# Block sums in the delta rule, scalings on one engine, and splits handed out as steps, in a hybrid decoder layer

## The chip, the core and the metric
The kernel runs on one core of one Trainium2 chip. The metric is device time in microseconds (us), the median of three runs: 1703.05 us before the change (1699.76 to 1704.30). Five engines work side by side, each through its own queue of instructions in order: TensorE (PE, with its weight loads shown apart as PEld), VectorE (DVE), ScalarE (ACT), GpSimd (POOL) and SyncE (SP), which here only issues DMA transfers.

## The reference
One layer on x (1024 tokens by 1024 channels, float32):

```python
proj = x @ w_in                                # q k v z beta a | NSA q, k/v, gates | merge gates
o_a  = gated_deltanet(...)                     # 4 heads, delta rule in chunks, state S 128x128
o_b  = native_sparse_attention(...)            # 8 heads of 64, 2 kv heads: compressed, selected, window
mixed = sigmoid(gate_a) * (o_a @ w_branch_gdn) + sigmoid(gate_b) * (o_b @ w_branch_nsa)
h    = layer_norm(alpha * x + mixed @ w_out)
u    = causal_dwconv(h @ w_up)                 # 2 x 2816 channels, 3 taps
f    = (silu(u_g) * u_v) @ w_down              # w_down: 2816 x 1024
out  = layer_norm(alpha * h + f)
```

The selected branch takes 16 blocks of 64 keys, and there are 16, so it is plain causal attention. Each of its softmaxes, and each of the window's, ends with P = exp(s - max) times a number per row, the gate divided by the row's sum.

## The kernel before
The stages follow one another in the trace: a first projection (0 to 60 us), the delta rule (60 to 593), attention (593 to 864), the branch products, merge and output projection (864 to 1104), the feed-forward part (1104 to 1655) and the last norm. Products take a float32 operand as two parts, high and low, one from a copy on ACT (`wh`, `oAh`, ...) and the other from a subtraction (`wl`, `oAl`, ...).

**Delta rule.** Eight iterations n = 0 to 7, each half a head (head n // 2, four chunks of 128 tokens). `pre` (L543) prepares a half: it forms `Am`, writes it to DRAM (`aimg`, L588), reads its diagonal blocks back as `AB` (L590), inverts them in small DVE instructions (L596 to L612, `pr`, `XB`), writes that to DRAM (`zimg`, L613) and reads it back as `Z` (L615), whose transpose `X` (L617) goes into the products `sm<-Z,Am` that follow. `scan` (L678) carries the state `S` from chunk to chunk (L703). Between these steps PE's order is filled with projections (`fills`, L759 to L772): `plan` names for each n its generators (`z_gen`, `act_gen`, `mix_gen`), each of which loads a weight block of 512 KB (L189), splits it on ACT and POOL (L183, L184), and gives 48 matmuls. `mix_gen` writes its result as `sig` to DRAM (L537).

**Attention.** Sixteen units (t, g), a tile of 128 queries by a kv head. For a unit `score_steps` (L945) makes scores and their exponentials `P` for branch b = 0 (selected) and 1 (window): DVE takes the row maxima (L979), ACT the exponentials with their sums (L981), and `fin` makes `rr` = gate / sum on DVE (`norm`, L942 and L943) and calls `scale` (L928) four times, once a head. `scale` goes round the letters of `SCALE = "GGGGGA"` (L926): G is a multiplication on POOL (L934), A one on ACT (L932). `cmp_scores` does the same for the compressed branch, `Pc`, always with POOL (L1010). `pv_steps` (L1013) turns P with PE (L1045), copies it out of PSUM as high part on ACT (L1052) and low part on DVE (L1053), and multiplies by `vS`; its end takes a buffer `tmp`, from ACT (L1029), and adds on DVE into `oB` (L1030). `weave` mixes the score steps of one unit with the product steps of the one before.

**Down sums.** The feed-forward part reads sums of blocks of w_down. `down_sums` (L1075) makes them and puts them into DRAM (`wsum`): a call finishes the block that the last call began (three POOL subtractions, L1079 and L1081, and two stores of 256 KB, L1083) and begins the next (two loads of 256 KB, L1090). There are 22 blocks; the attention loop calls it 25 times, once or twice a unit. Its buffers, `tmp`, the weight blocks and the mask tile `am` are all tiles "w" of the pool `stream`, a ring of three; `am` holds one of the three for all of attention.

**Splits of oA.** `gA` holds the result of the gated delta rule. `split_high` (L1106) copies it in eight pieces, four on ACT and four on DVE, and `split_low` (L1116) subtracts in eight pieces on POOL, before the branch products. Both are called in the attention loop, in the units (0, 0) and (0, 1), the loop's last two (`UNITS` has t = 0 at its end).

**What sets the order.** Only PE's instructions run in the order in which the program issues them (`MS`, L26). Those of DVE, ACT, POOL and SP are put in order by a scheduler that plays the program on a timeline of its own when the kernel is built, so the place of a call in the code doesn't by itself say where its instructions come in a queue.

Of the kernel before, what the change touches and what calls it, by code (L numbers as in the profile page):

```python
# [11 lines left out]
F32 = mybir.dt.float32  # L12
F32R = mybir.dt.float32r
# [134 lines left out]
def hybrid_block_kernel(ctx: ExitStack, tc: tile.TileContext, x, w_in, gdn_conv_w, gdn_a_log,  # L148
# [341 lines left out]
    sig = [dram.tile([128, T], F32, name=f"sig{j}") for j in range(16)]  # L490
    gd = tc.tile_pool(name="gdn", bufs=2)
    with gd as gp:
# [247 lines left out]
        with tc.manual_schedule(engines=MS):  # L740
# [186 lines left out]
    SCALE = "GGGGGA"  # L927
# [147 lines left out]
    def down_sums():  # L1075

        if held:
            b, k, cs = held.pop()
            G.tensor_tensor(b[:, 0:2], b[:, 1:4:2], b[:, 0:2], op=OP.subtract)  # L1079
            for o, x, y in ((3, 3, 0), (2, 2, 3)):  # L1080
                G.tensor_tensor(b[:, o], b[:, x], b[:, y], op=OP.subtract)  # L1081
            for r in range(2):
                nc.sync.dma_start(wsum[r][k].rearrange("p (h c) -> p h c", h=2)[:, :, cs], b[:, 2 * r:2 * r + 2, :])  # L1083
        if summed:
            k, c = divmod(summed.pop(0), 2)
            cs = slice(c * 256, c * 256 + 256)
            b = wtile().rearrange("p (b c) -> p b c", b=4)
            for r in range(2):
                src = w_down[(k + KD * r) * 128:(k + KD * r + 1) * 128, :].rearrange("p (h c) -> p h c", h=2)
                nc.sync.dma_start(b[:, 2 * r:2 * r + 2, :], src[:, :, cs])  # L1090
            held.append((b, k, cs))

# [13 lines left out]
    def split_high(src, nm_, pool, engines):  # L1106
        hi = oT[nm_, "hi"] = pool.tile([128, 4, T], F32R, name=f"o{nm_}h", tag="s")
        for hf, hs in enumerate(HS):
            oT[nm_, "h", hf] = hi[:, :, hs]
            for k in range(4):  # L1110
                if engines[k % len(engines)] is V:
                    V.tensor_copy(hi[:, k, hs], src[:, k, hs])
                else:
                    A.activation(hi[:, k, hs], src[:, k, hs], AF.Copy)

    def split_low(src, nm_, pool, engine):  # L1116
        hi = oT[nm_, "hi"]
        lo = pool.tile([128, 4, T], F32R, name=f"o{nm_}l", tag="s")
        for hf, hs in enumerate(HS):
            oT[nm_, "l", hf] = lo[:, :, hs]  # L1120
            for k in range(4):
                engine.tensor_tensor(lo[:, k, hs], src[:, k, hs], hi[:, k, hs].bitcast(F32), op=OP.subtract)
# [18 lines left out]
    with tc.manual_schedule(engines=MS):  # L1141
# [4 lines left out]
        for t, g in UNITS[1:]:  # L1146
            s = stats(t, g)
            down_sums()
            if (t, g) == (0, 0):
                split_high(gA, "A", S6, [A, V])  # L1150
            if (t, g) == (0, 1):
                load_ab(0, wtile)
                split_low(gA, "A", S6, G)
            weave(score_steps(s, 0), pairs[:n0])
            cmp_scores(s)
            if t > 2:
                down_sums()
            weave(score_steps(s, 1), pairs[n0:])
# [69 lines left out]
        split_high(oB, "B", S2b, [A, V])  # L1228
        split_low(oB, "B", S2b, V)
# [694 lines left out]
```

## Time and profile before

| | |
|---|---|
| median of three runs | 1703.05 us |
| profiled execution | 1698.21 us, span 1696.5 us, granted clock 0.992 |
| PE | busy 1660.5 us, 98% of the span |
| DVE, ACT, POOL | busy 1115.9, 734.3, 777.5 us |
| delta rule, 60 to 593 us | PE busy 531.84 of 533.00 |
| attention, 593 to 864 us | PE busy 257.32 of 271.00, DVE 233.94, ACT 210.97, POOL 186.23 |
| feed-forward, 1104 to 1655 us | PE busy 551.00 of 551.00 |

The windows view gives for a stretch each engine's busy time with the number of its instructions, and the clock that TensorE was granted as a share of full speed (PEclk). The timeline gives each instruction's start and length, and in brackets how long its engine stood idle ahead of it and which instruction, by engine, tile and line, ended that. An idle time on an engine that isn't the bottleneck costs nothing.

### The profile page before, as it was taken

The page shows a single profiled execution, that of the slowest core. Times are in us where ns is not written, and L with a number is a line of the kernel's source. Part 1 is how long each engine was busy: PE and PEld are TensorE (multiplying, and loading weights), DVE is VectorE, ACT ScalarE, POOL GpSimd, SP SyncE. Part 2 cuts the span into 40 slices and gives each one's busy share as a digit, 9 for nine tenths or more (in the row PEclk, how much of TensorE's full clock was granted, in tenths as well). Part 3 has the DMA queues.
Part 4 walks back from the last instruction along what each step waited for, and adds up shares of the span by engine and source line. Part 5 has one row for each costly group of instructions (what it writes and reads, how often), then busy time and mean ns, then how long its engine had stood idle before and what let it go on. Part 6 is the DMA issues. An engine that isn't in the chain of part 4 may idle for free.

```text
span 1696.5 us, 23194 instructions
## 1 busy us (share of the span) xinstructions
PE 1660.5 (98%) x8453; PEld 1391.9 (82%) x8453; DVE 1115.9 (66%) x2108; ACT 734.3 (43%) x1268; POOL 777.5 (46%) x630
## 2 busy tenths in 40 slices
PE   9999999999999999999899998999999999999997
PEld 9788888888888887888787887788888888888886
DVE  4555657567523478999853338997777677865657
ACT  3322322333223477888733215544444444444333
POOL 2322222222213647778647326778777777110005
PEclk9999999999999999999999999999999999999999
DMA  5222221212222313333036603334322332697722
GB/s 180 76 64 77 58 75 46 77 52 60 87 73 61 119 37 115 127 123 107 13 106 209 232 25 116 90 105 132 105 93 100 105 107 93 218 331 264 233 91 99
DMA packets 199022, 189.85 MB, mean 112 GB/s; under 512 B 19656, under 2 KB 155005, under 8 KB 198909
## 3 DMA queue, kind: packets, MB, share of 16 engines
q1 hardware_dynamic: 198909, 188.39, 34.3%
q8 instruction: 66, 1.08, 0.3%
q14 instruction: 47, 0.39, 0.1%
HBM read 136.97 MB, written 51.38 MB: 111 GB/s over the span
## 4 chain that ended last, share of the span: by engine, by line
PE 80%; DVE 9%; ACT 3%; issue 3%; POOL 2%; DMA 2%; SPq 0%; ACTq 0%; POOLq 0%; DVEq 0%
PE pq L194 35%; PE big L194 30%; PE sm L194 12%; DVE st L979 2%; PE sm L1045 1%; ACT P L981 1%; DVE wh L1053 1%; DVE wl L1053 1%; DVE st L943 1%; POOL P L934 1%; DMA w<-in_w_out_dram 0%; DVE wb L1516 0%; PE big L260 0%; POOL h L1373 0%; POOL h L1374 0%
## 5 line engine op out<-in xcount | busy, mean ns | idle before, releaser
L184 POOL TENSOR_TENSOR wl<-w,wh 128x1024 fp32r<-128x1024 f32 x48 | 115.9, 2417 | 361.2 <-PE big L194 138.6
L194 PE MATMUL big<-xTh,wh 128*128 128x512 f32 x608 | 244.4, 403 | 1.1 <-DVE sil L524 1.1
L194 PE MATMUL big<-xTl,wh 128*128 128x512 f32 x608 | 243.0, 400 | 0.0
L194 PE MATMUL pq<-wd 128*128 128x512 f32 x924 | 209.6, 389 | 0.0
L194 PEld LDWEIGHTS pq<-wd 128*128 128x128 f32 x924 | 173.4, 188 | 36.0
L194 PE MATMUL pq<-xb,wb 128*128 128x512 f32 x792 | 187.6, 391 | 2.1 <-DVE accs L1527 1.5
L1527 DVE SCALAR_TENSOR_TENSOR accs<-pq,fcw,accs 128x510 f32<-128x510 f32 (+3 forms) x264 | 144.5, 568 | 61.0 <-ACT accs L1615 56.3
L194 PEld LDWEIGHTS pq<-xb,wb 128*128 128x128 f32 x792 | 148.5, 188 | 34.9 <-issue 2.9
L194 PE MATMUL big<-xTh,wl 128*128 128x512 f32 x608 | 164.7, 401 | 0.0
L194 PEld LDWEIGHTS big<-xTh,wh 128*128 128x128 f32 x608 | 114.6, 189 | 21.8 <-ACT sil L521 1.5
L194 PEld LDWEIGHTS big<-xTl,wh 128*128 128x128 f32 x608 | 114.6, 189 | 20.5 <-issue 0.2
L194 PE MATMUL pq<-mTh,wb 128*128 128x512 f32 x528 | 126.3, 395 | 3.5 <-ACT mTh L1315 3.1
L194 PE MATMUL pq<-mTl,wb 128*128 128x512 f32 x528 | 127.4, 391 | 0.0
L194 PEld LDWEIGHTS big<-xTh,wl 128*128 128x128 f32 x608 | 109.9, 188 | 21.0
L934 POOL TENSOR_TENSOR P<-P,st 128x640 f32<-128x640 f32 (+6 forms) x94 | 106.4, 1161 | 42.7 <-DVE st L943 16.5
L194 PEld LDWEIGHTS pq<-mTh,wb 128*128 128x128 f32 x528 | 100.2, 190 | 25.7 <-ACT mTh L1315 3.3
L194 PEld LDWEIGHTS pq<-mTl,wb 128*128 128x128 f32 x528 | 99.1, 188 | 21.2
L1516 POOL TENSOR_TENSOR wb<-w,wb 128x512 fp32r<-128x512 f32 x79 | 103.6, 1317 | 27.5 <-ACT wb L1315 27.5
L183 ACT ACTIVATE wh<-w 128x1024 fp32r<-128x1024 f32 x48 | 50.5, 1058 | 115.7 <-PE big L194 62.6
L194 PE MATMUL big<-kS,qS 128*128 128x320 f32 (+5 forms) x384 | 87.6, 345 | 2.1 <-ACT P L981 1.8
L1315 ACT ACTIVATE wb<-w 128x512 fp32r<-128x512 f32 x85 | 53.3, 629 | 80.3 <-PE pq L194 75.9
L979 DVE TENSOR_REDUCE st<-big 128x1 f32<-128x640 f32 (+7 forms) x88 | 83.4, 947 | 6.4 <-PE big L194 6.1
(409 smaller groups left out, 3483.7 us busy)
## 6 DMA issues: line engine op xcount, KB each, us to landing
w<-in_w_in_dram SPq DMA_DIRECT2D x40, 512.0 KB, 3.8
w<-in_w_up_dram SPq DMA_DIRECT2D x36, 512.0 KB, 3.7
w<-in_w_down_dram SPq DMA_DIRECT2D x53, 256.0 KB, 3.8
wsum<-w SPq DMA_DIRECT2D x44, 256.0 KB, 2.4
sig<-th SPq DMA_DIRECT2D x32, 256.0 KB, 2.2
w<-sig SPq DMA_DIRECT2D x30, 256.0 KB, 3.2
wx<-in_w_up_dram SPq DMA_DIRECT2D x11, 512.0 KB, 3.8
gdrC<-accs SPq DMA_DIRECT2D x11, 512.0 KB, 2.6
```

The costliest lines, as they stand in the source:

```text
L183: A.activation(wh[:, :n], w[:, :n], AF.Copy)
L184: G.tensor_tensor(wl[:, :n], w[:, :n], wh[:, :n].bitcast(F32), op=OP.subtract)
L194: PE.matmul(o, a, b, start=start, stop=stop, skip_group_check=True)
L934: G.tensor_tensor(p, p, r.to_broadcast([128, p.shape[1]]), op=OP.mult)
L943: V.tensor_tensor(s["rr"][:, b], s["rr"][:, b], s["gt"][:, b], op=OP.mult)
L979: V.reduce_max(nm, pv if m > 1 else pv[:, 0], axis=AX.X, negate=True)
L981: A.activation(P[:, r0 + i, :n], pv[:, i], AF.Exp, bias=nm[:, i:i + 1], accum_out=su[:, i:i + 1])
L1045: PE.transpose(tp[:n, r * 128:(r + 1) * 128], P[:, r, c0:c0 + n], ident)
L1053: V.tensor_tensor(pl, tp[:n], ph.bitcast(F32), op=OP.subtract)
L1315: A.activation(o, i, AF.Copy)
L1516: e.tensor_tensor(H.tile[:, 1], src(), H.tile[:, 0].bitcast(F32), op=OP.subtract)
L1527: V.scalar_tensor_tensor(o, i, fcw[:, 2 - s, j:j + 1], o, op0=OP.mult, op1=OP.add)
```

## The change
Three parts. The program calls `down_sums` from the delta rule's fills, for n of 1 and more ahead of each generator (by the plan 4, 3, 4, 3, 3, 3, 3 and 2 calls, 25 in all, of which 23 have work), and no longer in the attention loop. `SCALE` becomes "G", so every scaling is a POOL instruction. And `split_high` and `split_low` return lists of steps, which for oA are strewn among the product steps of the same two units, in place of being called at once.

```diff
                 total = 48 * len(fills)
 
-                def chain(fills=fills):
-                    for f in fills:
+                def chain(fills=fills, n=n):
+                    for i, f in enumerate(fills):
+                        if n:
+                            down_sums()
                         yield from f()
...
-    SCALE = "GGGGGA"
+    SCALE = "G"
...
-    def down_sums():
-
-        if held:
-            b, k, cs = held.pop()
-            G.tensor_tensor(b[:, 0:2], b[:, 1:4:2], b[:, 0:2], op=OP.subtract)
-            for o, x, y in ((3, 3, 0), (2, 2, 3)):
-                G.tensor_tensor(b[:, o], b[:, x], b[:, y], op=OP.subtract)
-            for r in range(2):
-                nc.sync.dma_start(wsum[r][k].rearrange("p (h c) -> p h c", h=2)[:, :, cs], b[:, 2 * r:2 * r + 2, :])
...
     def split_high(src, nm_, pool, engines):
-        hi = oT[nm_, "hi"] = pool.tile([128, 4, T], F32R, name=f"o{nm_}h", tag="s")
-        for hf, hs in enumerate(HS):
...
+        return [functools.partial(f, hf, k) for hf in range(2) for k in range(4)]
...
+    def strewn(steps, more):
+
+        out, n = [], 0
+        for i, f in enumerate(steps):
+            out.append(f)
+            while n < len(more) and n * len(steps) < (i + 1) * len(more):
+                out.append(more[n])
+                n += 1
+        return out + more[n:]
...
             s = stats(t, g)
-            down_sums()
+            pa, pb = pairs[:n0], pairs[n0:]
             if (t, g) == (0, 0):
-                split_high(gA, "A", S6, [A, V])
+                pa = strewn(pa, split_high(gA, "A", S6, [A, V]))
+                lows = split_low(gA, "A", S6, G)
+                pb = strewn(pb, lows[:4])
             if (t, g) == (0, 1):
                 load_ab(0, wtile)
-                split_low(gA, "A", S6, G)
-            weave(score_steps(s, 0), pairs[:n0])
+                pa = strewn(pa, lows[4:])
+            weave(score_steps(s, 0), pa)
             cmp_scores(s)
-            if t > 2:
-                down_sums()
-            weave(score_steps(s, 1), pairs[n0:])
+            weave(score_steps(s, 1), pb)
```

PE's queue is the same, instruction for instruction, in both kernels. On SP, the queue at the delta rule's iteration n = 4, before: `w<-in_w_in_dram` is a weight block of a fill, `aimg` to `Z` are the four transfers of `pre`.

```order
L537 DMA sig_638<-th 128x512 x2
L189 DMA w<-in_w_in_dram 128x8x128
L588 DMA aimg_502<-Am 128x4x128
L590 DMA AB<-aimg_502 32x16x16
L189 DMA w<-in_w_in_dram 128x8x128
L613 DMA zimg_500<-XB 32x16x16
L615 DMA Z<-zimg_500 128x4x128
L537 DMA sig_639<-th 128x512 x2
```

The same stretch of SP's queue after the change, where `w<-in_w_down_dram` are the two loads of a block and `wsum_8` its two stores:

```order
L555 DMA sig_638<-th 128x512 x2
L506 DMA w<-in_w_down_dram 128x2x256 x2
L606 DMA aimg_502<-Am 128x4x128
L499 DMA wsum_8_618<-w 256x1x256
L499 DMA wsum_8_629<-w 256x1x256
L608 DMA AB<-aimg_502 32x16x16
L189 DMA w<-in_w_in_dram 128x8x128
L506 DMA w<-in_w_down_dram 128x2x256 x2
L631 DMA zimg_500<-XB 32x16x16
L633 DMA Z<-zimg_500 128x4x128
L499 DMA wsum_8_618<-w 256x1x256
L499 DMA wsum_8_629<-w 256x1x256
```

Two blocks' loads and stores have come in among the four transfers, one pair of stores between `aimg` and `AB`; such a pair, or one store of it, stands there for n = 1 to 5, and all 22 blocks are through before n = 6.

On ACT in the middle of attention, before (around 805 us), where `P<-P` at L932 is a scaling:

```order
L1052 ACTIVATE wh<-sm 128x512
L981 ACTIVATE P_7595,st<-big,st 128x640
L1052 ACTIVATE wl<-sm 128x512
L981 ACTIVATE P_7595,st<-big,st 128x640
L1052 ACTIVATE wh<-sm 128x512
L932 ACTIVATE P_7595<-P_7595,st 128x640
L1052 ACTIVATE wh<-sm 128x512
L981 ACTIVATE P_7696,st<-big,st 128x1024
```

The same stretch after:

```order
L1072 ACTIVATE wh<-sm 128x512
L1001 ACTIVATE P_7608,st<-big,st 128x640
L1072 ACTIVATE wl<-sm 128x512
L1001 ACTIVATE P_7608,st<-big,st 128x640
L1072 ACTIVATE wh<-sm 128x512 x2
L1001 ACTIVATE P_7701,st<-big,st 128x1024
```

The scaling is gone from between the copies. On POOL at the end of attention, before, where `oAl` are the low parts of oA:

```order
L934 TENSOR_TENSOR P_7852<-P_7852,st 128x640 x4
L934 TENSOR_TENSOR Pw<-Pw,st 128x128 x3
L1122 TENSOR_TENSOR oAl<-gA,oAh 128x512 x8
L1010 TENSOR_TENSOR Pc<-Pc,st 128x256
L934 TENSOR_TENSOR Pw<-Pw,st 128x128 x3
```

After:

```order
L954 TENSOR_TENSOR P_7852<-P_7852,st 128x640 x4
L954 TENSOR_TENSOR Pw<-Pw,st 128x128 x4
L1130 TENSOR_TENSOR oAl<-gA,oAh 128x512 x8
L1030 TENSOR_TENSOR Pc<-Pc,st 128x256
L954 TENSOR_TENSOR Pw<-Pw,st 128x128 x4
```

The eight low parts stand in one piece as before, between the same scalings, which are four and four in place of three and three. On ACT the four `oAh` copies, and on DVE the four casts, stand together at the same place as before too.

## Rows read from the trace of the kernel before

**Rows 1.** Windows: busy PE, PEld, DVE, ACT, POOL; PEclk; DMA share; GB/s

```profile
60.00:593.00 533.00, 531.84 (x2867) 446.73 (x2866) 293.45 (x770) 163.64 (x258) 144.78 (x85) 1.00 0.24 69
593.00:864.00 271.00, 257.32 (x1639) 223.93 (x1638) 233.94 (x414) 210.97 (x475) 186.23 (x194) 0.97 0.26 86
660.00:670.00 10.00, 7.83 (x32) 6.52 (x31) 5.74 (x11) 5.21 (x11) 9.55 (x10) 0.66 0.46 149
678.00:806.00 128.00, 124.96 (x834) 110.61 (x833) 121.18 (x204) 104.85 (x212) 103.12 (x96) 1.00 0.36 118
845.00:855.00 10.00, 8.36 (x39) 7.44 (x40) 5.20 (x9) 4.97 (x16) 7.01 (x10) 0.66 0.00 0
```

**Rows 2.** Timeline of attention: PE's waits, in brackets idle time and releaser

```profile
629.61 0.62 PE L194 MATMUL big<-kS,qS 128*128 128x384 f32 x2 [0.21 <-ACT P L981]
655.89 0.33 PE L1045 MATMUL sm<-ident,P 128*128 128x128 f32 x1 [0.56 <-POOL P L934]
662.70 0.60 PE L1045 MATMUL sm<-ident,Pc 128*64 128x128 f32 x4 [2.17 <-DVE oB L1030]
807.54 0.50 PE L194 MATMUL sm<-wh,vS 128*128 128x512 f32 x1 [0.84 <-DVE wh L1053]
821.72 0.85 PE L194 MATMUL big<-kS,qS 128*128 128x320 f32 x4 [0.17 <-ACT P L981]
830.81 0.73 PE L194 MATMUL sm<-wh,vS 128*128 128x512 f32 x2 [0.95 <-DVE wh L1053]
832.85 0.66 PE L1045 MATMUL sm<-ident,P 128*128 128x128 f32 x4 [1.30 <-DVE wl L1053]
846.64 0.50 PE L194 MATMUL sm<-wh,vS 128*128 128x512 f32 x1 [1.75 <-DVE wh L1053]
```

**Rows 3.** Timeline of ACT, POOL and DVE ahead of the wait at 662.70

```profile
659.01 1.54 POOL L1081 TENSOR_TENSOR w<-w 128x256 f32<-128x256 f32 x2
661.24 0.59 ACT L1029 ACTIVATE w<-sm 64x512 f32<-64x512 f32 x1 [2.14 <-POOL w L1081]
661.86 0.69 DVE L1030 TENSOR_TENSOR oB<-sm,w 64x512 f32<-64x512 f32 x1 [1.89 <-ACT w L1029]
```

**Rows 4.** Timeline of ACT: the scaling ahead of PE's wait at 807.54

```profile
805.85 0.83 ACT L932 ACTIVATE P<-P,st 128x640 f32<-128x640 f32 x1 [0.38 <-DVE st L943]
```

**Rows 5.** Groups by line, attention: busy us, mean ns; idle before, releasers

```profile
L932 ACT ACTIVATE P<-P,st 128x640 f32<-128x640 f32 (+6 forms) x18 | 14.2, 790 | 4.1 <-DVE st L943 4.0
L932 ACT ACTIVATE Pw<-Pw,st 128x128 f32<-128x128 f32 x3 | 1.2, 399 | 0.8 <-DVE st L943 0.8
L934 POOL TENSOR_TENSOR P<-P,st 128x640 f32<-128x640 f32 x34 | 41.6, 1256 | 11.1 <-ACT oAh L1114 4.9 <-DVE st L943 3.5 <-ACT wh L1052 2.7
L1081 POOL TENSOR_TENSOR w<-w 128x256 f32<-128x256 f32 x41 | 29.9, 738 | 0.8
L1079 POOL TENSOR_TENSOR w<-w 128x512 f32<-128x512 f32 x20 | 25.6, 1284 | 25.5 <-DMA w<-in_w_down_dram 11.7 <-DVE wh L1053 5.2 <-PE sm L1045 4.0
```

**Rows 6.** Timeline of the end of attention: ACT, POOL and DVE

```profile
827.36 2.19 ACT L1114 ACTIVATE oAh<-gA 128x512 fp32r<-128x512 f32 x4
837.28 9.92 POOL L1122 TENSOR_TENSOR oAl<-gA,oAh 128x512 fp32r<-128x512 f32 x8 [1.61 <-PE sm L1045]
844.89 1.10 DVE L943 TENSOR_TENSOR st<-st,gates 128x4 f32<-128x4 f32 x1
```

**Rows 7.** Timeline of iteration n = 4 of the delta rule: SP, DVE, PE

```profile
309.69 0.37 SPq L588 DMA_DIRECT2D aimg<-Am  x1
311.99 0.32 SPq L590 DMA_DIRECT2D AB<-aimg  x1
315.48 0.33 DVE L703 SCALAR_TENSOR_TENSOR S<-S,egl,sm 128x128 f32<-128x128 f32 x1
317.52 0.39 PE L194 MATMUL sm<-S,kc 128*128 128x128 f32 x2
328.96 0.71 DVE L617 STREAM_TRANSPOSE X<-Z 128x512 f32<-128x512 f32 x1 [2.40 <-DMA Z<-zimg]
335.41 1.08 PEld L194 LDWEIGHTS sm<-Z,Am 128*128 128x128 f32 x8
```

**Rows 8.** The page's DMA issues: KB each, median us from issue to landing

```profile
w<-in_w_down_dram SPq DMA_DIRECT2D x53, 256.0 KB, 3.8
wsum<-w SPq DMA_DIRECT2D x44, 256.0 KB, 2.4
```

**Rows 9.** One DVE line: instructions, shortest, median and longest in ns

```profile
L943 DVE TENSOR_TENSOR st<-st,gates x48: 150/166/1430, 606.0 to 860.8; 128x4 f32<-128x4 f32 x48
```

More of the change, by code (lines that the diff above doesn't have):

```diff
@@ L490, in hybrid_block_kernel, with down_sums @@
     sig = [dram.tile([128, T], F32, name=f"sig{j}") for j in range(16)]
+    def down_sums():
+        if held:
+            b, k, cs = held.pop()
+            G.tensor_tensor(b[:, 0:2], b[:, 1:4:2], b[:, 0:2], op=OP.subtract)
+            for o, x, y in ((3, 3, 0), (2, 2, 3)):
+                G.tensor_tensor(b[:, o], b[:, x], b[:, y], op=OP.subtract)
+            for r in range(2):
+                nc.sync.dma_start(wsum[r][k].rearrange("p (h c) -> p h c", h=2)[:, :, cs], b[:, 2 * r:2 * r + 2, :])
+        if summed:
+            k, c = divmod(summed.pop(0), 2)
+            cs = slice(c * 256, c * 256 + 256)
+            b = wtile().rearrange("p (b c) -> p b c", b=4)
+            for r in range(2):
+                src = w_down[(k + KD * r) * 128:(k + KD * r + 1) * 128, :].rearrange("p (h c) -> p h c", h=2)
+                nc.sync.dma_start(b[:, 2 * r:2 * r + 2, :], src[:, :, cs])
+            held.append((b, k, cs))
     gd = tc.tile_pool(name="gdn", bufs=2)
@@ L1073, in weave @@
             f()
-    def down_sums():
-        if held:
-            b, k, cs = held.pop()
-            G.tensor_tensor(b[:, 0:2], b[:, 1:4:2], b[:, 0:2], op=OP.subtract)
-            for o, x, y in ((3, 3, 0), (2, 2, 3)):
-                G.tensor_tensor(b[:, o], b[:, x], b[:, y], op=OP.subtract)
-            for r in range(2):
-                nc.sync.dma_start(wsum[r][k].rearrange("p (h c) -> p h c", h=2)[:, :, cs], b[:, 2 * r:2 * r + 2, :])
[L1084 to L1091, printed above, removed]
     pend = []
@@ L1106, in split_high, with f @@
     def split_high(src, nm_, pool, engines):
-        hi = oT[nm_, "hi"] = pool.tile([128, 4, T], F32R, name=f"o{nm_}h", tag="s")
-        for hf, hs in enumerate(HS):
-            oT[nm_, "h", hf] = hi[:, :, hs]
[L1110 to L1114, printed above, removed]
-    def split_low(src, nm_, pool, engine):
-        hi = oT[nm_, "hi"]
-        lo = pool.tile([128, 4, T], F32R, name=f"o{nm_}l", tag="s")
-        for hf, hs in enumerate(HS):
-            oT[nm_, "l", hf] = lo[:, :, hs]
-            for k in range(4):
-                engine.tensor_tensor(lo[:, k, hs], src[:, k, hs], hi[:, k, hs].bitcast(F32), op=OP.subtract)
+        def f(hf, k):
+            hs = HS[hf]
+            if not (hf or k):
+                oT[nm_, "hi"] = pool.tile([128, 4, T], F32R, name=f"o{nm_}h", tag="s")
+            hi = oT[nm_, "hi"]
+            oT[nm_, "h", hf] = hi[:, :, hs]
+            if engines[k % len(engines)] is V:
+                V.tensor_copy(hi[:, k, hs], src[:, k, hs])
+            else:
+                A.activation(hi[:, k, hs], src[:, k, hs], AF.Copy)
+        return [functools.partial(f, hf, k) for hf in range(2) for k in range(4)]
+    def split_low(src, nm_, pool, engine):
+        def f(hf, k):
+            hs = HS[hf]
+            if not (hf or k):
+                oT[nm_, "lo"] = pool.tile([128, 4, T], F32R, name=f"o{nm_}l", tag="s")
+            hi, lo = oT[nm_, "hi"], oT[nm_, "lo"]
+            oT[nm_, "l", hf] = lo[:, :, hs]
+            engine.tensor_tensor(lo[:, k, hs], src[:, k, hs], hi[:, k, hs].bitcast(F32), op=OP.subtract)
+        return [functools.partial(f, hf, k) for hf in range(2) for k in range(4)]
+    def strewn(steps, more):
[6 more added lines that the diff above has]
+        return out + more[n:]
     def load_ab(j, get):
@@ L1227, in hybrid_block_kernel @@
         flush()
-        split_high(oB, "B", S2b, [A, V])
-        split_low(oB, "B", S2b, V)
+        for f in split_high(oB, "B", S2b, [A, V]) + split_low(oB, "B", S2b, V):
+            f()
         for _ in y0:
```

## The prediction

> **What bounds the kernel now.** I read the page's busy shares first, then the windows by stage. In the delta rule TensorE (PE) is idle for 533.00 - 531.84 = 1.16 us, in attention for 271.00 - 257.32 = 13.68 us [rows 1]. In the feed-forward part it is never idle, by the table of the profile. So PE bounds the kernel. Its instructions are the same and in the same order after the change, so only its idle time, and time at a lower granted clock, can be won. All of the change's work before lay in attention, where there are 13.68 us of idle time and two stretches in which the granted clock is 0.66 on average, between its levels of 1.2 and 2.4 GHz [rows 1]: 10 us at 0.66 give away 10 x (1 - 0.66) = 3.4 us each. Attention thus holds 13.68 + 6.8 = 20.5 us at most.
>
> Next I read PE's waits there one by one in the timeline, and followed each back to what its releaser itself had waited for. They fall into groups:
> - Waits behind a scaling on ACT. The row of 807.54 shows one: PE waits 0.84 us for DVE's `wh` part, which waits for ACT's copy, and in front of that copy stands a scaling of 0.83 us that itself waited for `st` [rows 2, 4]. There are eight of these (0.21, 0.48, 0.28, 0.18, 0.72, 0.40, 0.84, 0.17; the first at 629.61, the last at 821.72), 3.28 us.
> - Waits behind the down sums. At 655.89 PE waits 0.56 us for a scaling on POOL that stood behind a subtraction of sums. At 662.70 it waits 2.17 us: it needs `oB`, that needs `tmp` on ACT (L1029), and `tmp` is a tile of the ring of three, of which the masks hold one, so it waits 2.14 us until POOL has finished a block of sums (L1081) [rows 2, 3]. Together 2.73 us. Behind this wait lies the first stretch of low clock, 660 to 670 us [rows 1]: PE had stood for 2.17 us before its clock fell.
> - The end of attention: 0.95, 1.30 and 1.75 us, together 4.00, and then the second stretch of low clock. Four `oAh` copies on ACT take 2.19 us in one piece, `oAl` takes POOL for 9.92 us in one piece, and during it the small DVE product L943 takes about a microsecond [rows 2, 6].
> - The remaining 13.68 - 3.28 - 2.73 - 4.00 = 3.67 us are small waits that the change doesn't touch.
>
> **Part by part.** *The sums leave attention.* POOL loses 29.9 + 25.6 = 55.5 us there [rows 5], and the ring's two free tiles are no longer taken by blocks, so `tmp` finds one. The 2.73 us go, and with them the 3.4 us of low clock behind them: -6.13 us. What is late next at 662.70 is POOL's scaling of `P`, which stood behind the same subtractions and so moves earlier too.
>
> *The scalings go to POOL.* 18 + 3 scalings leave ACT, 15.4 us of busy time and 4.9 us in which ACT stood waiting for `st` in front of the copies that PE wants [rows 5]. The 3.28 us go. On POOL they cost more: 14.2 x 1256 / 790 = 22.6 us by the two rows of 128x640, and 1.2 us for the three small ones, 23.8 us. With the sums gone POOL's busy time in attention falls to 186.23 - 55.5 + 23.8 = 154.5 of 271 us, so it has room. But a unit's four scalings now stand in a row on POOL wherever one went to ACT, and its last `P` comes up to 1.26 us later; and DVE, busy for 121.18 of 128.00 us between 678 and 806 us (95%) [rows 1], bounds what PE can be given. So part of the wait comes back. Bounds: nothing, and all 3.28 us. PE's only listed wait for a scaling on POOL was the one behind the sums, which is nearer to nothing; I take +1.0.
>
> The Trainium skill, SBUF — State Buffer, section Who interferes with whom, speaks against this part: a DVE instruction with two inputs in SBUF and a GpSimd instruction that reads SBUF lock each other out for a whole instruction, and "PE and ACT never wait on anyone". L943 has two such inputs and takes 166 ns at the median and 1430 at most [rows 9], where one scaling on POOL takes 1256 [rows 5], so the trace agrees; by the rule each of the 21 moved scalings can hold up DVE, the second busiest engine, and all 3.28 us would come back.
>
> *The splits of oA.* By the queues shown above, `oAh` on ACT and DVE and `oAl` on POOL stand in one piece at the same place as before. So this part does nothing, and the 4.00 us and the second low clock stay: 0. Bounds: a microsecond later, since one more scaling stands in front of `oAl`, or all of it gone (4.00 + 3.4), if the emptier queues let the copies run early.
>
> *The sums enter the delta rule.* 22 blocks of 1.284 + 2 x 0.738 = 2.76 us [rows 5], 60.8 us on POOL, which is busy for only 144.78 of 533 us there [rows 1], and 88 transfers on SP. Two chains can suffer.
> First, SP's queue: a block's stores now stand between `aimg` and `AB` in n = 1 to 5, and a store can't be issued before its block is subtracted; everything behind it waits, `AB` first. In n = 4 `AB` was issued 311.99 - 309.69 = 2.30 us after `aimg`, which is the time that `aimg` takes to land, and DVE, which runs its queue in order, has `S` ready at 315.48 + 0.33 = 315.81 where PE takes it at 317.52: 1.71 us to spare [rows 7]. If the block's load had landed when `aimg` was issued, the subtractions take 2.76 us, `AB` is late by 2.76 - 2.30 = 0.46 us, and nothing shows. That is the likely case, since the load is issued before `aimg` and the trace has 3.8 us for it [rows 8], while `aimg` itself waits for `Am` on DVE.
> Second, the inversion: DVE's some 25 small instructions from `AB` to `X` can meet a POOL subtraction each time. `X` is done at 328.96 + 0.71 = 329.67 and PE asks for it at 335.41, 5.7 us later [rows 7]; one block's 2.76 us are hidden, two as well (5.5).
> So the delta stage costs between nothing and the 12.8 us of the rival below; nearest to the rows is the covered case, and I take +0.5 for single waits.
>
> **The sum.** -3.28 - 2.73 - 3.4 + 1.0 + 0 + 0.5 = -7.9 us. The profiled execution took 1698.21 us (span 1696.5), so 1690.3; it is 4.84 us below the median of 1703.05, so on the median's scale 1690.3 x 1703.05 / 1698.21 = 1695.1. Its own range: without the returned wait and the delta stage's half microsecond -9.4, with all of the 3.28 back and two more in the delta stage -4.1, that is 1693.6 to 1698.9, and 2 us either side for the runs' own scatter (4.5 us between the three): 1691 to 1701.
>
> **Rivals.**
> - *The end of attention clears too.* POOL is emptier, ACT has no scalings, so the copies and `oAl` run where there is room: another 4.00 + 3.4 goes, 1695.1 - 7.4 = 1687.7. For it: the wait at 846.64 is for ACT and DVE work that gets shorter. Against: `oAl` keeps its 9.92 us in one piece between the same scalings.
> - *The waits come back on POOL and DVE.* With DVE at 95% PE may merely wait elsewhere; then only the ring's wait is won, and its low clock is met a few microseconds later by another wait. -2.73 - 3.28 + 3.28 - 0.3, about 3 us: 1700. For it: DVE's share. Against: the second low clock, like the first, follows waits of over 1 us, and the ones behind ACT are all below that.
> - *Slower: the stores on SP hold up `AB`.* If a block's load is issued only just ahead of `aimg`, because its tile or the stores in front of it come late, the store behind `aimg` waits 3.8 + 1.284 + 2 x 0.738 = 6.56 us, `AB` is late by 6.56 - 2.30 = 4.26, and over the 1.71 us to spare 2.55 us of PE are lost, in five iterations 12.8 us. Then -7.9 + 12.8 = +4.9: 1708. Its point of decision is a load that lands over 2.30 + 1.71 - 2.76 = 1.25 us after `aimg` is issued; beyond that every microsecond costs one. For it: SP's queue has three blocks in each iteration, where one wait stops the next fill's weights as well; with a fall of the clock behind waits of 2.55 us it could reach 1715. Against: the transfers fill a share of only 0.24 of that stage [rows 1], so a load has room to land early.
> - By the rule of the Trainium skill named above, in SBUF — State Buffer, Who interferes with whom, three blocks' subtractions met one after another by the inversion would hold it for 3 x 2.76 = 8.3 us, 2.6 more than its 5.7; in six iterations 15.6 us, 1711. No run here shows them together; I count it with the slower case.
>
> **How the numbers follow.** Forecast 0.60; clears too 0.08; comes back 0.21; slower 0.11. A measurement of this kernel can tell 0.3%, 5.1 us: faster is below 1697.9, slower above 1708.2. The forecast's own range reaches just past 1697.9, so of its 0.60 some 0.50 are faster; with 0.08 and 0.05 of the third case that is 0.63. Same: 0.10 of the forecast, 0.14 of the third case, 0.02 of the fourth, 0.26. Slower: 0.09 of the fourth and 0.02 of the third, where more comes back than was there, 0.11. The predicted time is 1695; the range, which leaves out the ends of the first and last rivals, is 1685 to 1707.
>
> **What would show it.** Right: no idle time of ACT at L1029 for a subtraction and a clock of 1.00 around 660 us; no scaling rows on ACT; POOL busy for some 154 us in attention; PE idle for 1 to 2 us in the delta rule; and the waits and the clock of 0.66 still at the end of attention. Wrong: PE waiting in the delta rule for `S` or `X` behind `AB` or `Z`, with SP's stores in front; or PE's waits for `wh`, `wl` and `P` in attention summing to 10 us again.

## The result and the profile after

The changed kernel takes 1709.79 us (median of 7 runs, 1706.11 to 1710.82) against 1700.16 us for the kernel before (7 runs). The ratio is 1.0055 with a 95% interval of 1.004 to 1.007: slower by more than the 0.3% that can be told, where faster was forecast. Attention became shorter, by somewhat more than was forecast; the loss is in the delta rule.

Since PE's queue is the same in both kernels, four of its instructions serve as marks: the first projection that waits for `sil` (66.57 us before, 67.85 after), the last product of the state, `sm<-S,kc`, and the first score, `big<-kS,qS`; the first branch product, `big<-oAh,wh`, ends attention.

| us between marks, by the timelines | before | after |
|---|---|---|
| first `sil` to last state product (delta rule) | 448.2 | 466.6 |
| last state product to first score | 84.7 | 84.7 |
| first score to first branch product (attention) | 258.0 | 246.7 |
| whole span | 1696.5 | 1704.4 |

+18.4 in the delta rule and -11.4 in attention, with +1.3 ahead of them and small change behind, make the +7.9 us of the two spans. The windows view of after, same columns as [rows 1], for the delta rule, for two stretches in it, and for attention (which lies some 20 us later now):

```profile
60.00:612.00 552.00, 537.03 (x2870) 448.94 (x2869) 311.69 (x772) 164.56 (x259) 203.95 (x145) 0.99 0.35 106
160.00:170.00 10.00, 6.21 (x23) 5.12 (x24) 9.79 (x38) 0.64 (x2) 3.86 (x4) 0.83 0.27 83
338.00:348.00 10.00, 8.06 (x34) 6.55 (x33) 3.78 (x8) 1.57 (x3) 2.83 (x3) 0.83 0.53 155
612.00:866.00 254.00, 244.74 (x1610) 215.44 (x1610) 226.47 (x403) 194.16 (x441) 152.40 (x149) 0.99 0.01 3
```

PE is idle for 552.00 - 537.03 = 14.97 us in the first of these, where it had 1.16 [rows 1], and its clock, 1.00 there before, is 0.83 on average in two stretches of 10 us, which gives away 1.7 us each. GpSimd (POOL) is busy for 152 us in attention, as worked out. PE's waits in the delta rule, from the timeline of after, with the releaser in brackets; all but the first (at 66.57 us it stood before too) are new:

```profile
67.85 0.47 PE L194 MATMUL big<-xTh,wh 128*128 128x512 f32 x1 [1.11 <-DVE sil L542]
163.79 0.79 PE L194 MATMUL sm<-S,kc 128*128 128x128 f32 x2 [4.10 <-DVE S L719]
229.08 0.49 PE L194 MATMUL sm<-S,kc 128*128 128x128 f32 x2 [1.94 <-DVE S L721]
273.41 0.49 PE L194 MATMUL sm<-S,kc 128*128 128x128 f32 x2 [1.31 <-DVE S L719]
288.04 0.49 PE L194 MATMUL sm<-vb,Z 128*128 128x128 f32 x2 [2.44 <-DVE vb L708]
340.17 0.49 PE L194 MATMUL sm<-S,kc 128*128 128x128 f32 x2 [1.94 <-DVE S L721]
381.83 0.49 PE L194 MATMUL sm<-S,kc 128*128 128x128 f32 x2 [0.42 <-DVE S L719]
390.67 0.49 PE L194 MATMUL sm<-S,kc 128*128 128x128 f32 x2 [1.71 <-DVE S L721]
```

The seven new ones are 13.86 us. Their releaser, VectorE (DVE), is only the last link. What it had waited for is seen in the timeline of n = 1, the longest of them. `Am` was done at 148.69 + 0.60 = 149.29; these rows follow:

```profile
148.69 0.60 DVE L603 SCALAR_TENSOR_TENSOR Am<-sm,sc,tmp 128x128 f32<-128x128 f32 x2
152.21 1.30 POOL L495 TENSOR_TENSOR w<-w 128x512 f32<-128x512 f32 x1 [5.20 <-DMA w<-in_w_down_dram]
153.53 0.56 SPq L499 DMA_DIRECT2D wsum<-w  x1
154.13 0.61 SPq L606 DMA_DIRECT2D aimg<-Am  x1
155.16 0.56 SPq L499 DMA_DIRECT2D wsum<-w  x1
156.89 0.33 SPq L608 DMA_DIRECT2D AB<-aimg  x1
158.78 1.91 DVE L618 TENSOR_TENSOR pr<-XB,AB 32x1 f32<-32x1 f32 x2 [2.28 <-DMA AB<-aimg]
163.47 0.27 DVE L719 COPY S<-sm 128x128 f32<-128x128 f32 x1
```

The reader is to see a chain of four engines. POOL waits 5.20 us for a block of w_down to land and subtracts from 152.21 to 153.51; only then can SyncE (SP) issue the block's first store, at 153.53; `aimg` is queued behind that store and goes out at 154.13, 4.84 us after `Am` was ready; `AB` follows at 156.89; VectorE starts the inversion at 158.78, and `S`, behind those small steps in VectorE's queue, is written at 163.47. In n = 4 it is the other order, `aimg` first and the two stores between it and `AB`. These rows answer to [rows 7]:

```profile
323.11 1.30 POOL L495 TENSOR_TENSOR w<-w 128x512 f32<-128x512 f32 x1 [1.53 <-DMA w<-in_w_down_dram]
323.38 0.38 SPq L606 DMA_DIRECT2D aimg<-Am  x1
324.43 2.51 SPq L499 DMA_DIRECT2D wsum<-w  x2
324.49 1.87 POOL L497 TENSOR_TENSOR w<-w 128x256 f32<-128x256 f32 x2
327.05 0.55 SPq L608 DMA_DIRECT2D AB<-aimg  x1
329.46 0.22 DVE L618 TENSOR_TENSOR pr<-XB,AB 32x1 f32<-32x1 f32 x2 [1.59 <-DMA AB<-aimg]
339.79 0.33 DVE L721 SCALAR_TENSOR_TENSOR S<-S,egl,sm 128x128 f32<-128x128 f32 x1
```

`AB` comes 3.67 us after `aimg` where it was 2.30, since the second store had to wait for POOL until 324.49 + 1.87 = 326.36, and it lands later too. The block itself had landed in time: POOL began on it at 323.11, before `Am` was done at 323.35.

The state product that waits here, at 340.17, isn't the one that [rows 7] show at 317.52. PE's queue is the same in both kernels, so its partner before the change can be found by counting: it is the next one, and its `S` stands behind the whole inversion in VectorE's queue. Before the change:

```profile
324.17 0.33 DVE L703 SCALAR_TENSOR_TENSOR S<-S,egl,sm 128x128 f32<-128x128 f32 x1
324.55 0.49 PE L194 MATMUL sm<-S,kc 128*128 128x128 f32 x2
```

That `S` was ready at 324.17 + 0.33 = 324.50 and PE took it at 324.55. There was 0.05 us to spare. The table gives for the eight iterations the time from the end of `Am` to VectorE's first use of `AB`, and what the products that now wait had to spare before the change, both worked out from such rows:

| n | 0 | 1 | 2 | 3 | 4 | 5 | 6 | 7 |
|---|---|---|---|---|---|---|---|---|
| before, us | 4.29 | 4.33 | 4.27 | 4.24 | 4.21 | 4.26 | 5.02 | 4.90 |
| after, us | 6.36 | 9.49 | 6.06 | 6.16 | 6.11 | 6.53 | 4.94 | 4.87 |
| to spare before, us | - | 2.27 | 0.05 | 2.27, 0.83 | 0.05 | 1.26, 0.06 | - | - |
| PE's new waits, us | none | 4.10 | 1.94 | 1.31, 2.44 | 1.94 | 0.42, 1.71 | none | none |

The delay is there in n = 0 to 5, where sums are made, and gone in n = 6 and 7, which have none. In n = 0 no state product is waiting yet. In n = 2, 4 and 5 `AB` is used 1.79, 1.90 and 2.27 us later, 5.96 together, and PE waits 6.01: with nothing to spare, PE pays all of the delay. In n = 1 and 3 more was to spare, and PE still waits 4.10 and 3.75 us for delays of 5.16 and 1.92. There VectorE lost time as well, beside POOL's weight splits (L184): the pair of products at 158.78, which takes 0.22 us at 329.46, took 1.91, and in n = 3 a product for `sil` took 2.37 us, of which more is said under e11.

At the end of attention PE's waits are unchanged, as forecast. The timeline of after:

```profile
817.49 0.50 PE L194 MATMUL sm<-wh,vS 128*128 128x512 f32 x1 [1.16 <-DVE wh L1073]
840.77 0.73 PE L194 MATMUL sm<-wh,vS 128*128 128x512 f32 x2 [0.95 <-DVE wh L1073]
842.80 1.07 PE L1065 MATMUL sm<-ident,P 128*128 128x128 f32 x4 [1.30 <-DVE wl L1073]
848.83 9.93 POOL L1130 TENSOR_TENSOR oAl<-gA,oAh 128x512 fp32r<-128x512 f32 x8 [2.86 <-PE sm L1065]
858.20 0.50 PE L194 MATMUL sm<-wh,vS 128*128 128x512 f32 x1 [1.76 <-DVE wh L1073]
```

The last three waits of PE here are those of [rows 2], and `oAl` stands in one piece of 9.93 us as in [rows 6]. The clock isn't quite as it was: it is 0.83 from 840 to 850 us, where [rows 1] have 0.66. The first row answers to the wait at 807.54 in [rows 2]; it has grown, though no scaling is left on ACT. ScalarE's (ACT) `tmp` at L1049 now waits 0.4 us in all attention, by its row there, where one of its waits alone was 2.14 [rows 3]:

```profile
L1049 ACT ACTIVATE w<-sm 64x512 f32<-64x512 f32 x15 | 8.9, 593 | 0.4
```

### The profile page after: what moved, and what is told of

Read it like the earlier page. It is cut to its first block, busy times and chain, and to the rows that moved or that the text cites. A ratio compares the mean times of both kernels' runs of the same rounds, so it can differ in the third digit from the quotient of the medians.

```text
span 1704.4 us, 23188 instructions
## 1 busy us (share of the span) xinstructions
PE 1659.8 (97%) x8453; PEld 1391.1 (82%) x8453; DVE 1129.9 (66%) x2108; ACT 721.3 (42%) x1247; POOL 804.8 (47%) x651
## 4 chain that ended last, share of the span: by engine, by line
PE 78%; DVE 10%; DMA 4%; issue 3%; POOL 3%; ACT 2%; SPq 0%; POOLq 0%; DVEq 0%; ACTq 0%
PE pq L194 35%; PE big L194 27%; PE sm L194 12%; PE sm L1065 3%; DMA w<-in_w_down_dram 1%; DVE pr L618 1%; DVE st L999 1%; DMA AB<-aimg 1%; POOL wl L184 1%; ACT P L1001 1%; DMA w<-in_w_out_dram 1%; DVE wb L1535 0%; DVE wh L1073 0%; POOL h L1392 0%; POOL h L1393 0%
## 5 line engine op out<-in xcount | busy, mean ns | idle before, releaser
L184 POOL TENSOR_TENSOR wl<-w,wh 128x1024 fp32r<-128x1024 f32 x48 | 115.1, 2401 | 264.1 <-PE big L194 82.4
L954 POOL TENSOR_TENSOR P<-P,st 128x640 f32<-128x640 f32 (+6 forms) x112 | 126.7, 1162 | 95.7 <-DVE st L963 32.4
L1001 ACT ACTIVATE P<-big,st 128x640 f32<-128x640 f32 (+6 forms) x112 | 83.3, 749 | 13.4 <-DVE st L999 12.6
```

The source lines that it names most:

```text
L184: G.tensor_tensor(wl[:, :n], w[:, :n], wh[:, :n].bitcast(F32), op=OP.subtract)
L954: G.tensor_tensor(p, p, r.to_broadcast([128, p.shape[1]]), op=OP.mult)
L1001: A.activation(P[:, r0 + i, :n], pv[:, i], AF.Exp, bias=nm[:, i:i + 1], accum_out=su[:, i:i + 1])
```

## The experiments

Each was timed in five rounds beside the kernel before on the same chip; "ratio" is to that kernel, whose median was 1698.2 to 1698.5 us there, 1.7 to 2.0 below that of the first section. So runs of different rounds are compared here by ratios and segments. The two segments are those of the first table, from one profile each.

| run | median us | ratio, 95% interval | delta rule | attention |
|---|---|---|---|---|
| e1 sums moved, alone | 1713.61 | 1.0087, 1.0066 to 1.0108 | 470.2 | 249.8 |
| e2 scalings on POOL, alone | 1703.64 | 1.0033, 1.0017 to 1.0049 | 448.3 | 260.1 |
| e9 splits, alone | 1698.19 | 0.9994, 0.9979 to 1.0009 | 448.2 | 254.0 |
| e3 after, sums not stored | 1702.89 | 1.002, 1.0006 to 1.0034 | 459.6 | 246.7 |
| e4 before, two stores ahead of AB | 1702.05 | 1.0014, 0.9999 to 1.003 | 451.2 | 258.2 |
| e5 after, aimg and AB issued by ACT | 1693.87 | 0.9977, 0.9963 to 0.9991 | 452.0 | 246.6 |
| e6 before, aimg and AB issued by ACT | 1699.33 | 1.0005, 0.9989 to 1.0022 | 448.0 | 257.3 |
| e7 after, sums late | 1703.69 | 1.0027, 1.0013 to 1.0041 | 453.7 | 249.9 |
| e8 before, no tmp | 1708.52 | 1.0055, 1.0035 to 1.0074 | 448.2 | 268.0 |
| e10 e5, a sixth of the scalings on ACT | 1693.99 | 0.9976, 0.9956 to 0.9995 | 450.4 | 249.7 |
| e11 e5, oA's high parts on POOL | 1690.85 | 0.995, 0.9928 to 0.9972 | 452.4 | 246.8 |

**The parts by themselves.** e1 is the kernel before with the move of `down_sums` only:

```diff
+                    for i, f in enumerate(fills):
+                        if n:
+                            down_sums()
                         yield from f()
```

> The kernel before with the first part alone: the 22 block sums are called from the delta rule's fills, the scalings stay five on GpSimd to one on ScalarE, the splits stay as they were. Theory: the loss of the change lies in the delta rule alone, so it is here in full (the trace after has about 18.4 us more between the first state product and the last than the trace before), and of the gain in attention only the ring's part is here (2.73 us of waits and 3.4 us of low clock), so about +12 us, 1712. Rival: the loss needs the scalings on GpSimd too; then at most +3, 1703.

It lost in full: 22.0 us in the delta rule, with the same seven waits, and won 8.2 in attention. The rival falls; the first part makes the whole loss.

e2 has the second part only:

```diff
-    SCALE = "GGGGGA"
+    SCALE = "G"
```

> The kernel before with the second part alone: every scaling on GpSimd, the sums stay in attention. Theory: the eight PE waits behind ScalarE's scalings (3.28 us) go, about 1 us of waits on GpSimd comes back, the ring's wait and both stretches of low clock stay: about -2 us, 1698. Rival: GpSimd, now with sums and all scalings in attention (186 + 8 us by its busy time), gives out P late and VectorE is locked out more: 1700 to 1703.

A miss for the forecast; the rival holds, the time a little over its range. The waits behind ACT's scalings were not the price of the letters alone: with the sums still on POOL, scalings queue behind subtractions. POOL's and PE's timeline of e2:

```profile
676.25 1.43 POOL L1081 TENSOR_TENSOR w<-w 128x256 f32<-128x256 f32 x2
677.63 4.05 POOL L934 TENSOR_TENSOR P<-P,st 128x512 f32<-128x512 f32 x4
681.73 0.67 PE L1045 MATMUL sm<-ident,P 128*128 128x128 f32 x4 [1.93 <-POOL P L934]
```

PE waits 1.93 us for the fourth of four scalings in a row, which began behind two subtractions. Between e1 and the kernel after, where no sums are in the way, the same move shortens attention by 249.8 - 246.7 = 3.1 us. Only 1.25 us of it is idle time of PE (10.51 and 9.26 us by the timelines); 1.7 us is low clock at the end of attention, 0.66 over 10 us in e1 and 0.83 in the kernel after.

e9 has the third part alone:

```diff
-            weave(score_steps(s, 0), pairs[:n0])
+                pa = strewn(pa, split_high(gA, "A", S6, [A, V]))
...
+            weave(score_steps(s, 0), pa)
```

> The kernel before with the third part alone: the splits of oA as steps strewn among the product steps. By the queues it puts nothing in another place, so 1698 to 1700 and the waits at the end of attention (0.95, 1.30, 1.75 us) as before. Rival: the pieces run earlier and the waits at the end of attention shrink, 1694 or less.

No change, and the waits at the end of attention are 0.95, 1.30 and 1.76 us. Its attention of 254.0 us against 258.0 in the profile of before has a shorter time at the low clock, and the medians agree: what one profile shows of a segment in attention is good to about 4 us.

**What in the moved sums costs.** Two theories: A, SP's queue, in which `aimg` and `AB` stand behind transfers that wait for POOL; B, POOL's subtractions themselves, which delay `rr` and the weight split on POOL and hold up VectorE. e3 takes the stores out of the delta rule and issues them at the start of attention:

```diff
-            for r in range(2):
-                nc.sync.dma_start(wsum[r][k].rearrange("p (h c) -> p h c", h=2)[:, :, cs], b[:, 2 * r:2 * r + 2, :])
...
+    for r in range(2):
+        for j in range(KD):
+            for e in range(2):
+                nc.sync.dma_start(wsum[r][j][:, e * 512:e * 512 + 512], kS[1][:, 0, 0, 0:512].bitcast(F32))
```

> The kernel after, with the blocks loaded and subtracted in the delta rule as there, but not stored from there: the 44 stores of sums are issued at the start of attention instead, from a key tile (so the sums that the feed-forward part reads are other numbers). GpSimd's work in the delta rule is the same, SyncE has no store between aimg and AB. Theory A (the stores on SyncE's queue hold up AB and so the state): PE's waits for S and vb in the delta rule, 13.9 us, fall to under 3 us, the clock doesn't fall there, about 1693. Theory B (the subtractions on GpSimd hold up VectorE and the small steps in between): the waits stay above 9 us, 1705 or more.

By its waits it spoke for B: 9.4 us are left, over the mark of 9. The clock did not fall, and the time lies between the two forecasts. Its timeline of n = 2 shows why it could not separate the two:

```profile
209.76 0.38 SPq L604 DMA_DIRECT2D aimg<-Am  x1
210.80 1.88 POOL L497 TENSOR_TENSOR w<-w 128x256 f32<-128x256 f32 x2
212.70 0.39 SPq L189 DMA_DIRECT2D w<-in_w_in_dram  x1
213.15 0.57 SPq L606 DMA_DIRECT2D AB<-aimg  x1
216.56 0.22 DVE L616 TENSOR_TENSOR pr<-XB,AB 32x1 f32<-32x1 f32 x2 [1.52 <-DMA AB<-aimg]
```

With the stores gone a weight block's load has come between `aimg` and `AB`. Its tile is the one that POOL is subtracting in, so it goes out at 212.70, just behind the end of the subtraction at 212.68, and holds `AB` as a store had. From `Am` to `AB`'s use it takes 6.83 us here.

e4 meant to make `AB` late without POOL:

```diff
             nc.sync.dma_start(full_image(ai), Am)
             AB = gp.tile([32, 16, 16], F32, name="AB", tag="AB", bufs=1)
+            for r in range(2):
+                nc.sync.dma_start(spare[r], Am.rearrange("p c i -> p (c i)"))
             nc.sync.dma_start(AB, diag_blocks(ai))
```

> The kernel before with two more stores of 256 KB (Am once more, to a DRAM tile that nobody reads) between aimg and AB on SyncE in all eight iterations: GpSimd has nothing to do with it. AB is issued at least 1.1 us later (0.55 us for each issue), and lands behind 512 KB of other transfers. Theory A: the spare time of 1.3 to 2.5 us is used up in some iterations, PE waits for S with 1 to 2 us in three or more of them, 1703 to 1708. Theory B: AB late by that much costs nothing, PE's waits in the delta rule stay at about 1 us, 1700.

Inconclusive: the dose was missed. `AB` went out 2.32 to 2.42 us after `aimg` in all iterations, since both stores are issued within the time in which `AB` waits for `aimg` anyway. From `Am` to `AB`'s use it took 4.4 to 4.7 us in n = 0 to 5 and 5.8 to 5.9 in the last two, 0.1 to 1.0 us more than before; there were two waits (0.95 and 1.33 us), and the delta rule was 3 us longer, though the ratio's interval still holds 1. It shows that two transfers which are ready put off the issue of `AB` by at most 0.12 us; those after the change are not ready.

e5 leaves every sum, load and store where the change put it, and takes `aimg` and `AB` off SP's queue (`A` is ScalarE):

```diff
-            nc.sync.dma_start(full_image(ai), Am)
+            A.dma_start(full_image(ai), Am)
...
-            nc.sync.dma_start(AB, diag_blocks(ai))
+            A.dma_start(AB, diag_blocks(ai))
```

> The kernel after, with aimg and AB issued by ScalarE instead of SyncE in the delta rule; sums, loads and stores stay where they are. Theory A, sharpened by the traces (everything that SyncE holds back, the store or the load behind a tile that GpSimd has not freed, holds back aimg or AB: from the end of Am to the first use of AB it takes 4.3 us before, and 6.4, 9.5, 6.1, 6.2, 6.1 and 6.5 us after in n = 0 to 5): this time is 4.3 to 4.8 us again in every iteration, PE's waits of 13.9 us in the delta rule fall below 3 us, its clock doesn't fall there, 1709.8 - 13.9 - 3.4 = about 1692. Theory B (GpSimd's subtractions delay rr, the weight split and VectorE's chain by themselves): the waits in n = 1 and 3 stay, about 7 us, 1702.

> The control for it: the kernel before with aimg and AB issued by ScalarE. ScalarE stands for 2.3 us at AB until aimg has landed, with 164 of 533 us busy in this stage. Both theories: about no change, 1698 to 1702; if what is queued behind AB on ScalarE is late for PE, up to 2 us in each of eight iterations, 1716.

This decides it. The same edit does nothing that can be told to the kernel before (e6), and brings the kernel after from a ratio of 1.0055 to one of 0.9977, which is 13 us; by the profiles' spans it is 12.7 (1704.4 to 1691.7), and the delta rule alone becomes 14.6 us shorter. The timeline of e5 in n = 1, where ACT issues the two (ACTq):

```profile
147.89 1.29 POOL L495 TENSOR_TENSOR w<-w 128x512 f32<-128x512 f32 x1 [2.01 <-DMA w<-in_w_down_dram]
148.47 0.38 ACTq L606 DMA_DIRECT2D aimg<-Am  x1
149.20 2.51 SPq L499 DMA_DIRECT2D wsum<-w  x2
150.80 0.32 ACTq L608 DMA_DIRECT2D AB<-aimg  x1
152.90 0.22 DVE L618 TENSOR_TENSOR pr<-XB,AB 32x1 f32<-32x1 f32 x2 [0.41 <-DMA AB<-aimg]
158.57 0.39 PE L194 MATMUL sm<-S,kc 128*128 128x128 f32 x2
```

SP still stands at the store until POOL is done, but `AB` no longer cares: the first state product at 158.57 does not wait. From `Am` to `AB`'s use it takes 4.3 to 4.7 us in n = 0 to 4 and 5.6 in n = 5. PE's waits in the delta rule are 2.2 us (the largest, 1.21, in n = 5), its clock is 1.00 throughout. Theory A holds, and B can't be the main cause: all the subtractions are still in the delta rule. VectorE's inversion, from its first use of `AB` to the last step of `XB`, is as slow as in the kernel after (11.3 to 11.7 us in n = 1, 3 and 5, where it took 9.6 to 9.8 before), and with `AB` on time what was to spare covers most of it. 452.0 us against 448.2 before leaves some 3.8 us, of which the waits explain 2.2; the rest stays open.

**Other places for the sums.** e7 calls `down_sums` twice a weight block in the last fills of the delta rule and in the projections behind it, and the last seven times in attention (the main lines of the edit):

```diff
+    def sums_in(gen, every=24):
+        for i, x in enumerate(gen):
+            if i % every == 0:
+                down_sums()
+            yield x
...
-        along(q_tile(0), iter(()))
+        along(sums_in(q_tile(0)), iter(()))
```

> The kernel after, with the sums called twice a weight block in the last fill of the delta rule and in the projections behind it (where no aimg or AB is under way but that of n = 7), and the last seven calls in the first units of attention; all scalings on GpSimd. Theory A: the delta rule is as before (448 us from the first to the last state product) apart from up to 2 us in n = 7, attention keeps most of its gain of 11 us, 1690 to 1694. Rival: two blocks beside each weight block in the ring of three starve the weights, PE waits for wh in the projections by some us each, 1700 or more.

The rival. `AB` is on time in n = 0 to 6, late in n = 7 alone (6.19 us from `Am`, two waits of 3.0 us together). But from the last state product to the first score it takes 93.3 us where it took 84.7: now weight loads stand behind stores, as this timeline of e7 shows:

```profile
596.76 3.90 SPq L499 DMA_DIRECT2D wsum<-w  x3
601.42 0.51 SPq L499 DMA_DIRECT2D wsum<-w  x1
604.04 0.37 SPq L189 DMA_DIRECT2D w<-in_w_in_dram  x1
609.01 0.51 PE L194 MATMUL sm<-xTh,wh 128*128 128x512 f32 x1 [3.69 <-ACT wh L183]
```

e8 took the ring's wait out of the kernel before:

```diff
-            A.activation(tmp, o[e], AF.Copy)
-            V.tensor_tensor(oB[...], o[m]..., tmp..., op=OP.add)
+            A.activation(ob, o[e]..., AF.Copy)
+            V.tensor_tensor(ob, o[m]..., ob, op=OP.add)
```

> The kernel before, with tmp left out: ScalarE copies one half of the sum straight into oB and VectorE adds the other half onto it, so the end of a unit needs no tile of the ring. Theory of the forecast: PE's wait of 2.17 us at 662.70 goes and with it the half clock behind it, 1700 - 2.2 - 3.4 = about 1694.5. Rival: the clock falls a few us later behind another wait, or the wait is taken over by GpSimd's scalings behind the same sums: 1698 to 1700.

Neither: slower by 10 us. The wait at 662.70 is gone, but with the ring free the scheduler begins the sums earlier, and they stand in front of POOL's scalings where attention starts. POOL in e8, and the wait of PE that ends it (before, the first subtraction there came at 624.63):

```profile
617.80 1.27 POOL L1078 TENSOR_TENSOR w<-w 128x512 f32<-128x512 f32 x1 [1.22 <-PE sm L1044]
619.02 0.62 POOL L1010 TENSOR_TENSOR Pc<-Pc,st 128x256 f32<-128x256 f32 x1
619.70 1.06 PE L1044 MATMUL sm<-ident,Pc 128*64 128x128 f32 x4 [1.90 <-POOL Pc L1010]
634.73 1.06 PE L1044 MATMUL sm<-ident,Pc 128*64 128x128 f32 x4 [3.00 <-POOL Pc L1010]
```

The clock cost more than the waits: it is 0.73 from 610 to 640 us, where it was 1.00 before. From the first score to the first branch product PE's idle time grew by 3.7 us, and the time given away by low clock by 8.5. So the ring was the cause of the wait at 662.70, as the prediction read it, but freeing it while the sums stay in attention doesn't pay.

**On top of e5.** e10 undoes the second part in e5:

```diff
-    SCALE = "G"
+    SCALE = "GGGGGA"
```

> The kernel of e5 (sums in the delta rule, aimg and AB issued by ScalarE) with the second part undone, one scaling in six on ScalarE again. Theory: with the sums out of attention a scaling on GpSimd is free and one on ScalarE costs the waits behind it (3.28 us by the forecast, 3.1 us between e1 and the kernel after), so attention is 249.8 us from the first score to the first branch product and the time 1697. Rival: the scalings make no difference, 1694; or GpSimd is better off without them, 1692.

Attention is 249.7 us as expected, 3.2 more than in e5, but the medians are alike (1693.99 and 1693.87), as the rival said: its delta rule happened to be 1.6 us shorter. A worth of 3 us is not settled by the runs.

e11 lets POOL copy oA's high parts in e5 (the main line of the edit):

```diff
-                pa = strewn(pa, split_high(gA, "A", S6, [A, V]))
+                pa = strewn(pa, split_high(gA, "A", S6, [G]))
```

> The kernel of e5 with all eight high parts of oA copied by GpSimd, none by ScalarE and VectorE. Theory: the waits of 0.95 and 1.30 us at the end of attention come from the four copies in one piece on each of these engines, they go, and the one of 1.76 us (behind the low parts on GpSimd) stays: 1691.5. Rival: GpSimd is late with the last scalings or locks VectorE out for longer, the waits there grow: 1695 or more.

The time is the lowest of all, 1690.85 us, but not for the reason given: the waits at the end of attention are 1.34, 1.48 and 1.90 us in place of 0.95, 1.30 and 1.76, and attention is as long as in e5 (246.8 and 246.6). The intervals of e5 and e11 overlap, so that it beats e5 is not shown. Both beat the kernel after. e11 beats the kernel before by 0.5%; e5 does by 0.23%, clear of its interval but less than the 0.3% named above.

Its profile shows something else. In n = 3 of the delta rule, with `AB` on time (4.64 us from `Am`), PE waits as long as in the kernel after:

```profile
274.60 2.36 POOL L184 TENSOR_TENSOR wl<-w,wh 128x1024 fp32r<-128x1024 f32 x1 [2.83 <-issue]
275.16 2.35 DVE L546 SCALAR_TENSOR_TENSOR sil<-th,sil 128x512 f32<-128x512 f32 x1
277.83 0.49 PE L194 MATMUL sm<-vb,Z 128*128 128x128 f32 x2 [2.44 <-DVE vb L708]
```

VectorE's `sil`, which stands in front of `vb`, began behind POOL's weight split and took 2.35 us. In e5 it began at 276.15, just ahead of the split at 276.17, took 0.65 us, and PE waited 0.16. So one of the seven new waits, 2.44 of the 13.86 us, needs no late `AB`; it hangs on which of the two engines comes first.

## Why the prediction was wrong

- *What bounds the kernel.* Right: PE in the same order, so that only idle time and low clock could change. The 18.4 us were lost as 13.9 us of waits, 3.4 us of low clock and a small remainder.
- *The sums leave attention*, -6.13: right. From the kernel before to e1 PE's idle time in attention fell by 3.2 us and the low clock behind 662.70 went, 3.4 us; a further 1.7 us of the 8.2 is neither.
- *The scalings go to POOL*, -3.28 + 1.0: the 3.1 us of the profiles agree by luck. The eight waits that it wanted to remove are still 2.04 of 3.28 us in the kernel after, and idle time fell by 1.25 us only. Its example was misread: the wait of 0.84 us at 807.54 is 1.16 both in e1, with a scaling on ACT in front of the copy, and in the kernel after, with none; there VectorE begins on `wh` when a reduction of 1.22 us (L999) ends. Alone the part was a loss (e2, 0.33%), so its gain also depends on the first part.
- *The splits*: right, nothing (e9), and the waits at the end of attention stayed. Attention in all: -11.4 where -8.4 was forecast; the profiles' spread there is about 4.
- *The sums enter the delta rule*, +0.5: this step failed, and with it the sign. It was measured at +18.4. The prediction took 1.71 us to be to spare, and said: "If the block's load had landed when `aimg` was issued, the subtractions take 2.76 us, `AB` is late by 2.76 - 2.30 = 0.46 us, and nothing shows. That is the likely case". In n = 4, the iteration that it read, that case came, and both sizes were wrong. `AB` was used 1.90 us later, since the subtractions took 326.36 - 323.11 = 3.25 us, the second store's issue came behind them, and `AB` landed later. And the spare time was read from the wrong product: the `S` of 317.52 stands early among the inversion's small steps, the next one behind all of them, and that had 0.05 us to spare. PE waited 1.94 us.
- The prediction also counted only the stores between `aimg` and `AB`, in n = 1 to 5. In n = 0, 1 and 3 a store stood in front of `aimg` itself and held it for 1.8, 4.8 and 1.6 us. (Its 60.8 us of subtractions are 22 x 2.76 = 60.7, which changes nothing.)
- *The rival on the slower side* had the queue right: a store on SP that waits for POOL, `AB` behind it, and VectorE's queue and `S` behind that. Its price was right by luck: 2.55 us in five iterations, 12.8 us, 1708 and up to 1715 with the clock, where 13.9 us in five iterations, 3.4 for the clock and 1709.8 were measured. Its condition, a load that lands over 1.25 us after `aimg` is issued, is not what happened. In n = 0, 2, 3 and 4 POOL began on the block before `Am` was done, in n = 5 0.21 us after `aimg` was issued; by the condition n = 2, 4 and 5 would have lost nothing, and they lost 6.01 us. Only n = 1 had a late load, on which POOL began 2.92 us after `Am` was done, and there the store in front of `aimg` passed the delay on.
- *The rival by the Trainium skill*, SBUF — State Buffer, section Who interferes with whom: a VectorE instruction with two inputs in SBUF and a GpSimd instruction that reads SBUF contend, under an exclusive lock. The trace agrees that it happens: the pair at 158.78 took 1.91 us beside a weight split that ended at 160.60, and the `sil` of e11 took 2.35 beside one of 2.36. It has a part in the waits of n = 1 and 3. But e5 keeps every subtraction and loses 3.8 us at most in the delta rule, so it isn't what made most of this loss; that its time, 1711, is close to the measured one is luck.

## What to carry to other kernels

A queue in order makes whatever waits in it a wait for everything behind it: ask of each transfer that is moved not what it costs, but what it waits for when it reaches the head, and which critical transfer stands next. Two transfers that were ready put off the issue of `AB` by at most 0.12 us (e4); stores that waited for another engine, or a load that waited for a tile, made its use 1.8 to 5.2 us late. If a short critical round trip through DRAM shares a queue with bulk work, try another engine's queue for it (e5): two words in the code were worth some 13 us here.

When time to spare is read from a trace, it has to be that of every later instruction that hangs on the same chain, not of the first one that is found. Here one product had 1.71 us and the next 0.05.

## What the runs showed that had not been expected

- Freeing a buffer made the kernel 10 us slower (e8): the scheduler used the room to place the sums earlier, in front of scalings for which PE waited.
- Low clock does not follow every wait: in e3 eight waits with a sum of 9.4 us, none over 1.78, left the clock at 1.00 in the whole delta rule; after the change it fell twice, in the stretches of the waits of 4.10 us and of 1.94 at 340.17, while the 1.94 at 229.08 lies in a stretch, 170 to 338 us, at 1.00.
- ACT as issuer of `aimg` and `AB` cost nothing that can be told (e6, 1.0005, interval 0.9989 to 1.0022), though `AB` waits 2.3 us for `aimg` in ACT's queue each time.
